# W1's half columns by token, with seven half products for eight, in a GLA and sliding-window decoder trunk on one core

## The chip, the core and the metric

The kernel runs on one core of a Trainium2 chip. The core has five engines with instruction queues of their own: TensorE (PE; its weight loads are shown apart as PEld), VectorE (DVE), ScalarE (ACT), GpSimd (POOL) and SyncE (SP). Weights come from DRAM through 16 DMA engines; transfers are issued from the queues of SP, ACT and POOL. The metric is the time of one execution on the device in microseconds (us).

## The reference

Two layers over 256 tokens of width 2048, fp32: a gated linear attention layer, then a sliding-window attention layer, each followed by an MLP of width 8192 with a squared relu. The change is in the MLPs:

```python
def sqrelu_mlp(h, w1, w2):
    u = jax.nn.relu(h @ w1)
    return (u * u) @ w2

def reference(x, norm_mix, norm_mlp, mlp_w1, mlp_w2, ...):
    h = x
    for layer in range(DEPTH):
        u = rmsnorm(h, norm_mix[layer])
        ...
        h = h + sqrelu_mlp(rmsnorm(h, norm_mlp[layer]), mlp_w1[layer], mlp_w2[layer])
    return h
```

## The kernel before

**Precision.** Every product of fp32 matrices is made of three matmuls in float32r: each operand is split into a rounded high part and the rest, and high x high, high x low and low x high are summed in PSUM. For weights `halve` (L105) does it: of a block of 512x512, held as [128, 4, 512] in `ws`, ACT casts two halves into `wh`, and DVE subtracts them into `wl`. This page calls such a pair of operations of one half "a cast". There are four `wh` halves and three `wl` and `ws` buffers, so the casts can be two blocks ahead of PE.

**The MLP.** `mlp` (L939) goes through the 8192 hidden columns in four groups of 2048 (`g`). In a group W1 comes first, in four pieces of 512 columns (`c`), by `gemm_wide` (L188): the weights are stationary, the 256 tokens move, with high and low part of the activations side by side, so that there are matmuls of 512 columns (high weights) and of 256 (low weights), 16 of each for a block of 512 rows of W1. The result has the hidden columns on the partitions. `evac_u` (L1136) sums, applies relu and the norm's scale `rb2`, and squares; for pieces 2 and 3 it splits the result into high and low part (`us`), for pieces 0 and 1 `combine` (L962) makes seven combinations of the token halves (`op`).

**Seven half products for eight.** W2 then comes in two `seven`s (L986), each for 1024 output columns. Of its rows, those of pieces 2 and 3 are multiplied plainly (`plain`: four blocks, 24 matmuls of 512 columns each). Those of pieces 0 and 1 form a 2x2 matrix of 512x512 blocks against a 2x2 matrix of token halves and row blocks, and are multiplied in seven half products (12 matmuls each) instead of eight, from sums of blocks and of activations. Sums of weight blocks are made in two ways: a DMA on POOL's queue that adds while it writes (`more`, L1002), or a sum on DVE. The same scheme stands in class `Seven` (L215) for the attention's V and R products and its output projection. There the steps run in an order given as a string: `1` to `7` are half products, `e` reads out two accumulators, and two digits such as `21` are a plain block (row block, column block). The seven products use the operands `es`, made from high and low parts by `combine_act` (L916) and `combinations` (L706).

In `Seven`, product 1 loads block (0,0) into `wx` (two halves of 512 KB), and `load_x` (L238) then adds block (0,1) onto it by two DMAs on POOL's queue, as soon as product 1's casts have read it. Product 5 uses that sum, and `load_x` adds block (1,1) for product 6. Product 3 loads (1,1) into `y`, product 7 sums it with (0,1) on DVE. Product 2 loads (1,0), which DVE adds to `wx` for product 4.

**Order.** The program is recorded step by step. `later(n, fn)` puts a function off until `n` calls of `tick` have passed (L70 to L78); blocks and products tick. Loads and casts are recorded with a priority that lets them move ahead of other work (`tc.high_priority`, L109); the framework's scheduler then fixes one order per engine. Each engine runs its instructions in that order and waits for semaphores of the others. PSUM has eight banks: four under the tag `acc`, two `tp`, two `ms`. The pool `actp` has eight buffers for activations; four hold the MLP's input (`act[0]` to `act[3]`, 512 model columns each) and four a group's `op` and `us`.

## Time and profile before

| what | us |
|---|---|
| median of three runs | 2032.58 |
| lowest and highest of them | 2032.13, 2032.89 |
| span of the profiled execution | 2031.4 |
| one group of an MLP (452.90 to 623.57) | 170.67 |
| of it: a wide piece of W1, four times | 22.19 |
| of it: a `seven` of W2, twice | 40.80 |

The profile is of one execution; its span runs from the first to the last instruction, and the medians of the runs are 1.2 us above it, which is what lies around a span. PE's granted clock is 1.00 throughout. In the profile's lists a row such as `L81 PE MATMUL acc<-wh,act` names the line, the engine, the operation, and the tiles written and read; in a chain or a timeline the first number is the start in the span and the second the length. A matmul's listed length is longer than its share of the pipeline, so the pace of matmuls is read from starts.

### The profile page before, as it was taken

What the parts mean: (1) busy time and instruction counts of PE and PEld (TensorE: products, weight loads), DVE (VectorE), ACT (ScalarE), POOL (GpSimd) and SP (SyncE); (2) the same over time, 40 slices, a digit from 0 to 9 for tenths busy, and PEclk for the clock granted to TensorE, in tenths of its full rate; (3) what the DMA queues carried; (4) which work ended last, traced back from release to release, by engine and by line L of the source; (5) the groups of instructions that cost most, each with busy time, mean ns of one, the idle gap of its engine ahead of it and who ended that gap; (6) DMA issues with size and microseconds to landing.
All of it is one profiled execution on the core that took longest, in us unless ns stands there. A gap on an engine that the chain in (4) does not pass through costs nothing.

```text
span 2031.4 us, 26969 instructions
## 1 busy us (share of the span) xinstructions
PE 2020.5 (99%) x10566; PEld 1715.5 (84%) x10566; DVE 1547.7 (76%) x1796; ACT 1203.8 (59%) x1638; POOL 162.4 (8%) x175
## 2 busy tenths in 40 slices
PE   9999999999999999999999999999999999999999
PEld 9988888888888888888888878788888888888887
DVE  6688787867876876786798676876876786787777
ACT  6746666656555655555567677655655555555555
POOL 2251110000000000000001121000000000000000
PEclk9999999999999999999999999999999999999999
DMA  8445876676875785786676543775785786687575
GB/s 286 146 156 177 227 208 200 194 251 184 261 236 187 228 267 189 203 253 219 187 220 186 165 146 126 198 257 188 227 268 188 203 253 221 186 256 231 187 223 148
DMA packets 219280, 423.15 MB, mean 208 GB/s; under 512 B 7328, under 2 KB 17840, under 8 KB 219152
## 3 DMA queue, kind: packets, MB, share of 16 engines
q1 hardware_dynamic: 194496, 376.73, 54.4%
q0 software_dynamic: 21568, 42.81, 12.3%
q10 hardware_dynamic: 3088, 1.88, 0.3%
q8 instruction: 83, 1.36, 0.3%
q14 instruction: 45, 0.37, 0.0%
HBM read 419.29 MB, written 2.10 MB: 207 GB/s over the span
## 4 chain that ended last, share of the span: by engine, by line
PE 91%; DVE 2%; issue 2%; DMA 2%; ACT 2%; SPq 0%; ACTq 0%; POOL 0%; POOLq 0%; DVEq 0%
PE acc L81 58%; PE ms L81 22%; PE tp L81 10%; DMA wx<-in_b_w_o_dram 1%; ACT sc L1283 1%; DVE wl L115 1%; PE tp L831 0%; DMA ws<-in_a_w_in_dram 0%; PE tp L1215 0%; DVE sc L1293 0%; DMA xt<-in_x_dram 0%; DVE st L1277 0%; PE tp L701 0%; ACT wh L114 0%; DVE qhl L1246 0%
## 5 line engine op out<-in xcount | busy, mean ns | idle before, releaser
L115 DVE TENSOR_TENSOR wl<-ws,wh 128x1024 fp32r<-128x1024 f32 x600 | 739.6, 1241 | 276.7 <-ACT wh L114 273.4
L114 ACT CAST wh<-ws 128x1024 fp32r<-128x1024 f32 x600 | 629.2, 1052 | 451.9 <-PE acc L81 286.6
L81 PE MATMUL acc<-wh,act 128*128 128x512 f32 x1696 | 543.9, 394 | 0.5 <-ACT act L339 0.5
L81 PE MATMUL acc<-act,wh 128*128 128x512 f32 (+1 forms) x1536 | 453.3, 358 | 0.7 <-ACT wh L401 0.7
L81 PEld LDWEIGHTS acc<-wh,act 128*128 128x128 f32 x1696 | 317.4, 188 | 68.6 <-issue 2.0
L81 PE MATMUL acc<-act,wl 128*128 128x256 f32 x1280 | 355.3, 279 | 0.4 <-DVE wl L402 0.2
L81 PE MATMUL acc<-wl,act 128*128 128x512 f32 x848 | 330.3, 390 | 0.0
L81 PEld LDWEIGHTS acc<-act,wh 128*128 128x128 f32 x1536 | 272.1, 189 | 44.0 <-ACT wh L401 0.9
L115 DVE TENSOR_TENSOR wl<-wx,wh 128x1024 fp32r<-128x1024 f32 x160 | 193.5, 1222 | 82.7 <-ACT wh L114 80.5
L114 ACT CAST wh<-wx 128x1024 fp32r<-128x1024 f32 x160 | 168.0, 1054 | 134.2 <-PE acc L81 76.7
L81 PEld LDWEIGHTS acc<-act,wl 128*128 128x128 f32 x1280 | 241.4, 189 | 2.4 <-DVE wl L402 1.0
L81 PE MATMUL tp<-act,wh 128*128 128x512 f32 x528 | 204.5, 392 | 0.9 <-DVE wh L518 0.9
L81 PE MATMUL ms<-act,wh 128*128 128x512 f32 x512 | 201.7, 394 | 0.0
L81 PEld LDWEIGHTS acc<-wl,act 128*128 128x128 f32 x848 | 159.4, 188 | 32.6 <-issue 1.4
L81 PE MATMUL ms<-wh,act 128*128 128x512 f32 x512 | 163.5, 390 | 0.0
L81 PE MATMUL ms<-act,wl 128*128 128x256 f32 x512 | 143.4, 280 | 0.0
L1004 POOL DMA_DIRECT2D wx<-in_mlp_w_dram x32 | 41.2, 1287 | 1265.5 <-DVE wl L115 1251.1
L81 PE MATMUL tp<-act,wl 128*128 128x256 f32 x512 | 141.1, 276 | 0.0
L81 PE MATMUL acc<-wh,op 128*128 128x512 f32 x384 | 123.4, 389 | 0.0
L81 PE MATMUL acc<-wh,ops 128*128 128x512 f32 (+1 forms) x392 | 123.2, 386 | 0.0
L81 PEld LDWEIGHTS tp<-act,wh 128*128 128x128 f32 x528 | 99.1, 188 | 24.2 <-DVE wh L518 1.2
L81 PEld LDWEIGHTS ms<-act,wh 128*128 128x128 f32 x512 | 95.7, 187 | 21.5
(278 smaller groups left out, 2551.6 us busy)
## 6 DMA issues: line engine op xcount, KB each, us to landing
ws<-in_mlp_w_dram SPq DMA_DIRECT2D x224, 1024.0 KB, 5.3
ws<-in_a_w_in_dram SPq DMA_DIRECT2D x42, 1024.0 KB, 5.1
wx<-in_mlp_w_dram POOLq DMA_DIRECT2D x32, 1024.0 KB, 9.0
wx<-in_mlp_w_dram SPq DMA_DIRECT2D x16, 1024.0 KB, 5.0
wy<-in_mlp_w_dram SPq DMA_DIRECT2D x16, 1024.0 KB, 7.5
ws<-in_b_w_q_dram SPq DMA_DIRECT2D x16, 1024.0 KB, 5.0
ws<-in_a_w_o_dram SPq DMA_DIRECT2D x15, 1024.0 KB, 5.1
ws<-in_b_w_o_dram SPq DMA_DIRECT2D x15, 1024.0 KB, 5.0
```

The costliest lines, as they stand in the source:

```text
L81: nc.tensor.matmul(o, lhsT=l, rhs=r, start=start, stop=stop, **kw)
L114: nc.scalar.copy(out=wh[:, js, :o], in_=w)
L115: nc.vector.tensor_sub(out=wl[:, ks, :o], in0=w, in1=wh.bitcast(F32)[:, js, :o])
L1004: nc.gpsimd.dma_start(out=ws, in_=block(i, j).rearrange("(k p) n -> p k n", p=P), accum_op=ALU.add)
L1283: nc.scalar.activation(out=sc[:, h], in_=sc[:, h], func=AF.Exp, bias=nmx[:, h:h + 1], scale=f[:, h:h + 1], accum_out=su[:, h:h + 1])
```

## The change

The first two pieces of W1 in each group are no longer made by `gemm_wide`. A new function `first_two` runs class `Seven` over them, with the tokens on the partitions: W1's rows of `act[0]` and `act[1]` go plainly, those of `act[2]` and `act[3]` in the seven half products (`skip=2` turns the row blocks by two). The four results (two token halves, two pieces) get relu and the norm's scale on ACT, are transposed by PE (`turn`: four 128x128 blocks each) and squared by ACT on the way back to `uf`.

The operands `es` from the activations are the same in all four groups. In the first group `combine_act` makes them at two ticks inside `first_two`, and SP writes them to two DRAM tiles (`kept`); in the other three groups two DMAs on POOL's queue read them back. `combine` for W2's operands is put off into piece 2. The first group has an order of its own, `FIRST`; the others use the second of `ORDERS`.

```diff
+FIRST = "21 31 1 20 30 3 7 e 5 6 2 4"
...
         def block(self, i, j):
-            return self.at(i, j).rearrange("(k p) n -> p k n", p=P)
+            return self.at((i + self.skip) % NC4, j).rearrange("(k p) n -> p k n", p=P)
...
         def p7(self, after):
             b12 = self.load(0, 1)
             with tc.high_priority(offset=WPRI):
                 nc.vector.tensor_add(out=b12, in0=b12, in1=self.y)
-            after["p7"](self.product("C", self.op(3), b12))
+            late = "C" in self.banks
+            after["p7"](self.product("D" if late else "C", self.op(3), b12))
+            if late:
+                self.banks.pop("D")
...
-    def combine_act(es, act, b, room):
+    def combine_act(es, act, b, room, cs=(0, 1)):
...
-        for c in range(2):
+        for c in cs:
...
+        dp = mx.enter_context(tc.tile_pool(name="dp", bufs=1, space=bass.MemoryType.DRAM))
+        kept = [dp.tile([P, 2, 2, 4, P], F32, name=f"kept{i}") for i in range(2)]
...
+        def first_two(g, uf):
+            pairs = [actp.tile([P, 2, 2, 4, P], F32R, name="cmb", tag="act") for _ in range(2)]
+            es = [a[:, i] for a in pairs for i in range(2)]
+            if g:
+                for a, o in zip(pairs, kept):
+                    with tc.high_priority(offset=WPRI):
+                        nc.gpsimd.dma_start(out=a.bitcast(F32), in_=o)
+            else:
+                for b in range(2):
+                    later(RS + 1 + 2 * b, lambda b=b: combine_act(es, act, b, room, (2, 3)))
+
+                def keep():
+                    for a, o in zip(pairs, kept):
+                        nc.sync.dma_start(out=o, in_=a.bitcast(F32))
+                later(RS + 4, keep)
...
+            def relu(o, i, t):
+                nc.scalar.activation(out=o, in_=i, func=AF.Relu, scale=r[:, t:t + 1])
+
+            def turn(c, t, h):
+                tp = bank([P, 4, P], "tp")
+                for k in range(4):
+                    nc.tensor.transpose(out=tp[:, k, :], in_=h[:, k * P:(k + 1) * P], identity=ident)
+                nc.scalar.activation(out=uf[c][:, :, t * P:(t + 1) * P], in_=tp, func=AF.Square)
+
+            def p56(p):
+                add(v, p, v)
+                add(x12, ef[0], v)
+                relu(x12, x12, 0)
+                later(1, lambda: turn(1, 0, x12))
+                if not g:
+                    add(x21, x21, x22)
+                sub(x22, v, x22)
+                add(x22, ef[1], x22)
+                relu(x22, x22, 1)
+                later(2, lambda: turn(1, 1, x22))
+                sub(x21, x21, v)
...
+            z = Seven(lambda i, j: w1[i * C:(i + 1) * C, g * D + j * C:g * D + (j + 1) * C], act, es,
+                      [x[:, 2 * i:2 * i + 2] for i in range(2)],
+                      lambda: mp.tile([P, 4, C], F32, name="wy", tag="wy", bufs=1), 2)
...
+                   "a": p2, "c": p4}, ORDERS[1] if g else FIRST)
...
         for g in range(4):
             w = w2[g * D:(g + 1) * D]
             us, op, uf = {}, None, {}
...
-            for c in range(NC4):
-                if c >= 2:
-                    us[c] = new_act()
-                elif c == 0:
-                    op = new_ops()
+            first_two(g, uf)
+            op = new_ops()
+            for odd in range(2):
+                later(3 + odd, lambda odd=odd, op=op, uf=dict(uf): combine(op, odd, uf))
+            later(1, lambda: pause(1))
+            for c in (2, 3):
+                us[c] = new_act()
```

What stands in the engines' rows now is seen at three places, all in the first group of the first layer's MLP. The first is PE. Before, a wide piece of W1 stood there (`acc` are its accumulators, `act` the activations, `wh` and `wl` the cast weights):

```order
L81 MATMUL acc_3728<-act_3396,wh_3797 128x512
L81 MATMUL acc_3728<-act_3396,wl_3798 128x256
L81 MATMUL acc_3729<-act_3396,wh_3797 128x512
L81 MATMUL acc_3729<-act_3396,wl_3798 128x256
L81 MATMUL acc_3726<-act_3760,wh_3837 128x512
```

Now, on PE, from the end of product 5 (`wh_4009`) through product 6 (`wh_4030`, `wh_4031`) into product 2 (`wh_4061`); `cmb_3725` holds the sums of activations, `tp_4007` is their accumulator:

```order
L82 MATMUL tp_4007<-wh_4009,cmb_3725 128x512
L82 MATMUL tp_4007<-wh_4030,cmb_3725 128x512
L82 MATMUL tp_4007<-wl_4032,cmb_3725 128x512
L82 MATMUL tp_4007<-wh_4030,cmb_3725 128x512 x2
L82 MATMUL tp_4007<-wl_4032,cmb_3725 128x512
L82 MATMUL tp_4007<-wh_4030,cmb_3725 128x512
L82 MATMUL tp_4007<-wh_4031,cmb_3725 128x512
L82 MATMUL acc_3826<-wh_4061,act_3672 128x512
L82 MATMUL tp_4007<-wl_4032,cmb_3725 128x512
```

All are matmuls of 512 columns with the weights moving, and product 6 follows product 5 directly, with one matmul of product 2 ahead of its last third. The second place is DVE. Before, in the middle of the second wide piece, it had casts alone:

```order
L115 TENSOR_TENSOR wl_4039<-ws_4035,wh_4038 128x1024
L115 TENSOR_TENSOR wl_4080<-ws_4076,wh_4078 128x1024
L115 TENSOR_TENSOR wl_4080<-ws_4076,wh_4079 128x1024
L115 TENSOR_TENSOR wl_4157<-ws_4153,wh_4155 128x1024
L115 TENSOR_TENSOR wl_4157<-ws_4153,wh_4156 128x1024
```

Now, on DVE, from just before product 5's cast (`wl_4010`) to product 2's (`wl_4063`); `e`, `m` and `cmb` are `combine_act`'s sums, `wx_3727` the block that the DMAs add to:

```order
L714 TENSOR_TENSOR e_3914<-m_3911,e_3913 128x256
L116 TENSOR_TENSOR wl_4010<-wx_3727,wh_4008 128x1024
L714 TENSOR_TENSOR cmb_3725<-e_3913,cmb_3725 128x256
L116 TENSOR_TENSOR wl_4010<-wx_3727,wh_4009 128x1024
L714 TENSOR_TENSOR cmb_3725<-e_3913,cmb_3725 128x256
L714 TENSOR_TENSOR cmb_3726<-e_3914,cmb_3726 128x256 x2
L116 TENSOR_TENSOR wl_4032<-wx_3727,wh_4030 128x1024
L981 TENSOR_TENSOR h_3729<-h_3729,h_3728 128x512
L324 TENSOR_TENSOR wx_3727<-wx_3727,ws_4057 128x1024
L116 TENSOR_TENSOR wl_4032<-wx_3727,wh_4031 128x1024
L116 TENSOR_TENSOR wl_4063<-ws_4057,wh_4061 128x1024
```

The sums of activations stand between the casts, and the cast of product 6 (`wl_4032`), which needs the block that was added to, stands ahead of those of products 2 and 4. The third place is POOL's queue. Before, behind the norm's power came W2's accumulates alone:

```order
L347 TENSOR_TENSOR rstd_2917<-rv_3765,mhalf_103 128x2
L1004 DMA wx_4524<-in_mlp_w2_dram 128x4x512 x2
L1004 DMA wx_4814<-in_mlp_w2_dram 128x4x512 x2
L1004 DMA wx_5875<-in_mlp_w2_dram 128x4x512 x2
L1004 DMA wx_6165<-in_mlp_w2_dram 128x4x512 x2
```

Now, on POOL, through the first group and into the second:

```order
L352 TENSOR_TENSOR rstd_2917<-rv_3766,mhalf_103 128x2
L245 DMA wx_3727<-in_mlp_w1_dram 128x2x512 x3
L1078 DMA wx_4531<-in_mlp_w2_dram 128x4x512 x2
L1078 DMA wx_4821<-in_mlp_w2_dram 128x4x512 x2
L967 DMA cmb_5111<-kept0_3723 128x2048
L967 DMA cmb_5112<-kept1_3724 128x2048
L245 DMA wx_5115<-in_mlp_w1_dram 128x2x512 x4
```

Each group has four accumulating DMAs of W1 more (one of the first group's stands ahead of the power), and from the second group on two reads of `kept` stand behind the last accumulates of the group before.

## The prediction

> **What bounds the kernel now.** First the page's head, with the busy shares by engine, and its fourth part, the chain of work that ended last, by engine.

> ```profile
> span 2031.4 us, 26969 instructions
> PE 2020.5 (99%) x10566; PEld 1715.5 (84%) x10566; DVE 1547.7 (76%) x1796; ACT 1203.8 (59%) x1638; POOL 162.4 (8%) x175
> ...
> PE 91%; DVE 2%; issue 2%; DMA 2%; ACT 2%; SPq 0%; ACTq 0%; POOL 0%; POOLq 0%; DVEq 0%
> ```

> TensorE (PE) is busy for 99% of the span and is 91% of that chain. So time goes only where PE gets less to do, and comes only where PE is made to wait. Next the chain in order of time over one group of 2048 MLP columns (start, length, what), and the same stretch as windows (span; then busy time of PE, weight loads, DVE, ACT, POOL; granted clock, DMA share, GB/s).

> ```profile
> 452.90 22.19 PE acc L81 x128
> ...
> 500.03 13.60 PE ms L81 x60
> ...
> 452.90:475.09 22.19, 22.19 (x129) 19.57 (x129) 17.02 (x23) 13.32 (x21) 0.00 (x0) 1.00 0.58 190
> ...
> 500.03:540.83 40.80, 40.80 (x182) 33.78 (x181) 35.74 (x34) 25.03 (x26) 2.58 (x2) 1.00 0.77 243
> ```

> A wide piece, 512 columns of W1, is 128 matmuls in 22.19 us, without a gap. Sixty matmuls of 512 columns take 13.60 us: 0.2267 us each. The last row is one `seven` of W2: four plain blocks of 24 matmuls and seven half products of 12, together 180, and 180 x 0.2267 = 40.8. It too has no gap, though DVE is busy for 35.74 us of it. `first_two` has the same 180 matmuls and nearly the same casts and sums.

> **What goes.** Two wide pieces per group, 2 x 22.19 = 44.38 us of PE, become 40.80: 3.58 us less, in eight groups (four per layer) 28.6 us. The two pieces' evacuation on ACT and DVE goes too, off the path.

> **What comes on PE.** Four `turn`s of four fp32 transposes per group. The nearest rows are the residual's transposes between full matmuls (start, length, what).

> ```profile
> 1055.37 0.60 PE L831 MATMUL tp<-ident,xs 128*128 128x128 f32 x4
> 1055.73 0.48 PE L81 MATMUL ms<-wh,act 128*128 128x512 f32 x1
> ...
> 1058.59 0.60 PE L831 MATMUL tp<-ident,xs 128*128 128x128 f32 x4
> ```

> From one four to the next are 3.22 us, and twelve matmuls between them are worth 2.72: 0.5 us for four. At least it is the 0.36 us to the next start, at most four times the 0.27 us of a single one, 1.1. I take 0.5, the steady figure: 2.0 us per group, 16.0 in all (bounds 11.5 and 35). PE alone thus gives 28.6 - 16.0 = 12.6 us, 0.62%, if nothing waits.

> **What comes in an MLP's first group.** Here the order is `FIRST`: ... 3 7 e 5 6 2 4. Product 5 casts `wx`, then `load_x` adds block (1,1) onto it with two DMAs on POOL's queue, and product 6 casts the sum. `FIRST` puts 5 and 6 side by side, where the residual keeps two plain blocks (20 and 30) between them. What that interval is worth is seen in the second residual: the POOL issue, ACT's cast of product 6, DVE's work behind it, and the view of L243 with its landings.

> ```profile
> 1314.31 2.44 POOL L243 DMA_DIRECT2D wx<-in_b_w_o_dram  x2 [21.07 <-DVE wl L115]
> ...
> 1326.17 1.05 ACT L114 CAST wh<-wx 128x1024 fp32r<-128x1024 f32 x1 [4.08 <-DMA wx<-in_b_w_o_dram]
> ...
> 1315.43 10.64 DMA wx<-in_b_w_o_dram
> ...
> DMA to landing us min/median/max: 5.8/6.3/10.6
> ...
> wx<-in_b_w_o_dram POOLq DMA_DIRECT2D x2, 512.0 KB, 8.4
> ```

> ACT waited 4.08 us for the second half's landing, 10.6 us after its issue, although two blocks (10.9 us of PE) stood between; two megabytes of weights were on their way beside it. In the new order nothing stands between, and 2 MB of sums on their way to `kept` are beside it: the situation of these rows, so I take their median, 8.4 us, with 5.8 and 10.6 as ends.

> When does the accumulate start? DVE carries more in this group, since `combine_act` of chunks 2 and 3 stands between product 1 and product 5. Its operations by their rows (line, shapes, count; busy, mean ns):

> ```profile
> L115 DVE TENSOR_TENSOR wl<-wx,wh 128x1024 fp32r<-128x1024 f32 x160 | 193.5, 1222 | 82.7 <-ACT wh L114 80.5
> L114 ACT CAST wh<-wx 128x1024 fp32r<-128x1024 f32 x160 | 168.0, 1054 | 134.2 <-PE acc L81 76.7 <-PE ms L81 34.9 <-DMA wx<-in_mlp_w_dram 8.2
> L925 DVE TENSOR_TENSOR xu<-act 128x512 f32<-128x512 f32 x8 | 5.5, 686 | 3.2 <-PE ms L81 2.1 <-PE tp L701 1.0
> L709 DVE TENSOR_TENSOR xe<-xu,xe 128x256 f32<-128x256 f32 x12 | 5.0, 419 | 0.0
> L319 DVE TENSOR_TENSOR wx<-wx,ws 128x1024 f32<-128x1024 f32 x8 | 9.8, 1226 | 0.3
> L1085 DVE TENSOR_TENSOR wy<-wy,ws 128x2048 f32<-128x2048 f32 x16 | 36.6, 2286 | 0.1
> ...
> 1320.79 0.68 DVE L896 TENSOR_TENSOR xs<-acc,xs 128x512 f32<-128x512 f32 x1
> 1321.39 0.68 DVE L896 TENSOR_TENSOR xs<-tp,xs 128x512 f32<-128x512 f32 x1
> ```

> Operations in a row start 0.08 us sooner than their lengths add up (1320.79 to 1321.39 is 0.60, not 0.68), so a cast counts 1.14, a 512-wide sum 0.60, a 256-wide one 0.34, the sum of two whole blocks 2.2. From the start of product 1 up to the first half of product 5's cast DVE has eight casts (9.1), four sums of 512 (2.4), twelve of 256 (4.1), two rows of `along` (0.4) and one whole-block sum (2.2): 18.2 us. PE has product 1 and two plain blocks in that time, 2.72 + 10.88 = 13.6. So the cast ends 4.6 us after PE starts product 3. Without backlog it would wait only for a `wh` buffer: half a product (1.36), ACT's cast (1.05), its own (1.14), 3.6 us.

> From there: landing 4.6 + 8.4 = 13.0; ACT casts till 14.05; then DVE has, in its order, six casts, two `wx` sums and one sum of 512 up to the last cast of product 4 (8 x 1.14 + 0.60 = 9.7, till 23.8), and PE the five matmuls behind that (1.1): 24.9. Six products in a row would be 16.3. **PE loses 8.6 us**, 4.9 with the early cast and the shortest landing (3.6 + 5.8 + 1.05 + 9.7 + 1.1 - 16.3), 10.8 with the longest. Wide piece 2 then finds its buffers empty: DVE owes its first two casts, a sum and one cast of the next block (3 x 1.14 + 0.60 = 4.0 us), PE has 2.5 us (the five matmuls and eight of the wide piece): 1.5 us more, bounds 0 and 3. Together 10.1 per first group, **20.2 us** in both layers.

> **What comes in the other groups.** There 20 and 30 stand between 5 and 6 and the path stays PE's. In 6 2 4 DVE has six sums of 512 (3.6 us) beside its casts and `wx` sums; counted in the same way, the sum of `x21`, which frees the fourth accumulator bank, ends some 0.5 us after PE wants it behind product 4. With the transposes' relu on ACT I take 0.6 (0 to 2): 3.6 us in six groups. `combine` now stands wholly in piece 2 (eleven operations of 0.60 = 6.6 us). With 8 casts (9.1) and six late sums (3.6) DVE has 19.3 us there beside 24 of PE: hidden; without that cover it would cost up to 6.6 per group. The reloads of `kept` on POOL's queue wait for PE's last use of `us`, at the latest the end of the last plain block of the group before; three products, two plain blocks and product 1 (8.2 + 13.6 = 21.8 us) run before product 3 reads them.

> ```profile
> ws<-in_mlp_w_dram SPq DMA_DIRECT2D x224, 1024.0 KB, 5.3
> wx<-in_mlp_w_dram POOLq DMA_DIRECT2D x32, 1024.0 KB, 9.0
> ...
> 408.50:430.70 22.20, 22.20 (x135) 19.62 (x134) 14.83 (x23) 12.39 (x22) 0.72 (x1) 1.00 0.98 343
> ```

> A megabyte on that queue took 9.0 us (on SP's 5.3), so they cost nothing. The further 2 MB of weights per group also hide: 12 MB in 42.8 us are 280 GB/s, and the last row shows 343 with PE full. Writing `kept` stands on SP's queue between two weight loads and is ready for both soon after product 5's cast; nothing on PE waits for the write alone.

> **The sum.** -28.6 + 16.0 + 20.2 + 3.6 = +11.2 us on the profiled 2031.4. The median of the runs, 2032.58, is 1.2 us above that span, which is taken along: 2043.8, say **2044 us**, +0.6%. It is slower by two waits that the first groups buy with a gain meant for all eight.

> **Rivals.** (1) *The accumulate lands early.* With the early cast, a landing of 5.8 and no backlog behind it, a first group waits 4.9: 9.8 + 16.0 - 28.6 + 0 = -2.8, 2030 us; with 3.6 for the later groups 2033. For it: half of the L243 landings are under 6.3. Against: twelve small sums stand ahead of the cast in DVE's order. [...]

> (2) *Product 6 is covered, and the change is faster.* One mechanism, at the step from 5 to 6: if cast plus landing fit under the products still queued, the sum is -12.6 + 0 to 4, 2020 to 2024 us. It decides at 4.2 us per first group: more, and what is left of 12.6 is within 0.2% (4.1 us, about what a measurement of this kernel tells from no change). Cast plus landing would have to be 7.2 us (7.2 + 1.05 + 9.7 + 1.1 - 16.3 = 2.7, and 1.5 behind it); the shortest by the rows is 9.4.

> (3) *The wait grows.* If weights land late in the six other groups as well (their two reloads beside 10 MB of blocks), say two loads by 1.2 us, it is 14 us more: 2058. It begins where a block takes longer than the three products that it is asked for ahead, 8.2 us; the median is 5.3. Or PE's clock falls: every row above has it at 1.00, and PE nowhere stands still for long. With half the clock over products 6, 2 and 4 (5.44 us each for the 3.3 at which DVE feeds them) the two first groups would lose some 4.3 each: 2052. [...] No row here can show it.

> **Chances.** My sum 0.58, with a range of its own from 2037 to 2052; (1) 0.17; (2) 0.08; (3) 0.17. So faster by over 0.2% 0.08, within it 0.17, slower 0.75. For 8 in 10 the range leaves (2) out and the end of (3): 2030 to 2060, which also holds the first groups' waits from 4.9 to 10.8 + 3.

> **What would show it.** In the profile after: a group but the first takes some 169.7 us instead of 170.7 (3.58 less, 2.0 for transposes, 0.6 of waiting); in each first group the chain leaves PE between products 5 and 4, with the DMA to `wx` and then a row of DVE casts, some 10 us together; the POOL landing there is near 8 us; the four transposes stay near 0.5 us. It is wrong if PE goes through 5 6 2 4 without a gap, if the groups' period falls by far less than 1 us, or if waits on `cmb` show at product 3 of later groups.

## The result, and the profile after

The changed kernel takes 2051.26 us (median of four runs, 2050.33 to 2054.12) where the kernel before takes 2032.74: a ratio of 1.0093, with a 95% interval from 1.0078 to 1.0107. It is slower, as forecast, by 18.5 us instead of 11.2. Its profiled execution took 2050.72, with a span of 2049.0, which is 17.6 above the span before. The head of the page and its fourth part, the chain by engine:

```profile
span 2049.0 us, 26361 instructions
PE 2020.6 (99%) x10082; PEld 1694.0 (83%) x10082; DVE 1641.3 (80%) x1862; ACT 1267.2 (62%) x1694; POOL 208.9 (10%) x219
...
PE 89%; DMA 3%; DVE 3%; ACT 2%; issue 2%; SPq 0%; POOL 0%; ACTq 0%; POOLq 0%; DVEq 0%
```

PE's busy time has not moved (2020.6 for 2020.5), although it has 484 matmuls fewer: a half clock and slower wide pieces, both shown below, fill most of what they left. In the chain PE has lost two per cent, and DMA and DVE have gained one each. Where the time went is seen from the starts of one landmark, the sixty `ms` matmuls in the first `seven` of each group (chain of work, after):

```profile
513.01 13.60 PE ms L82 x60
...
682.15 13.60 PE ms L82 x60
...
852.02 13.60 PE ms L82 x60
...
1021.17 13.60 PE ms L82 x60
...
1454.17 13.60 PE ms L82 x60
...
1623.32 13.60 PE ms L82 x60
```

| landmark of group | before | after | later by | this group's share |
|---|---|---|---|---|
| layer 1, first | 500.03 | 513.01 | 12.98 | +12.45 (0.53 was there ahead of the MLP) |
| second | 670.69 | 682.15 | 11.46 | -1.52 |
| third | 841.35 | 852.02 | 10.67 | -0.79 |
| fourth | 1012.01 | 1021.17 | 9.16 | -1.51 |
| layer 2, first | 1432.21 | 1454.17 | 21.96 | +12.80 |
| second to fourth | 1944.19 (fourth) | 1961.60 | 17.41 | -1.52 each |
| end | 2031.4 | 2049.0 | 17.6 | |

The two first groups cost 25.3 us, and the six others bring back 8.4. In the first group of layer 1 PE's timeline shows the waits, in brackets with who ended them; the first row is the start of product 3, the last that of wide piece 2:

```profile
433.63 0.39 PE L82 MATMUL acc<-wh,cmb 128*128 128x512 f32 x1
...
438.30 0.50 PE L82 MATMUL acc<-wh,cmb 128*128 128x512 f32 x1 [1.35 <-ACT cmb L720]
...
446.92 0.50 PE L82 MATMUL tp<-wh,cmb 128*128 128x512 f32 x1 [3.10 <-ACT h L1021]
...
453.36 0.79 PE L82 MATMUL tp<-wh,cmb 128*128 128x512 f32 x1 [3.82 <-ACT wh L115]
...
462.58 0.39 PE L82 MATMUL acc<-act,wh 128*128 128x512 f32 x1
```

Products 3, 7, 5, 6, 2 and 4 take 28.95 us where their matmuls are worth 16.3: 12.65 lost. The two long waits are at the two halves of product 6, and behind both stands the accumulating DMA: first the rows of POOL and SP, then ACT's, then DVE's.

```profile
438.64 1.21 POOL L245 DMA_DIRECT2D wx<-in_mlp_w_dram  x1 [19.19 <-DVE wl L116]
440.10 1.20 POOL L245 DMA_DIRECT2D wx<-in_mlp_w_dram  x1 [0.26 <-DVE wl L116]
...
440.17 1.01 SPq L974 DMA_DIRECT2D kept<-cmb  x2
...
444.85 1.04 ACT L115 CAST wh<-wx 128x1024 fp32r<-128x1024 f32 x1 [6.29 <-DMA wx<-in_mlp_w_dram]
...
446.27 0.59 ACT L1021 COPY h<-tp 128x512 f32<-128x512 f32 x1
452.26 1.04 ACT L115 CAST wh<-wx 128x1024 fp32r<-128x1024 f32 x1 [5.40 <-DMA wx<-in_mlp_w_dram]
...
453.33 1.23 DVE L116 TENSOR_TENSOR wl<-wx,wh 128x1024 fp32r<-128x1024 f32 x1 [4.45 <-ACT wh L115]
454.48 1.22 DVE L116 TENSOR_TENSOR wl<-ws,wh 128x1024 fp32r<-128x1024 f32 x1
...
460.15 2.45 DVE L116 TENSOR_TENSOR wl<-ws,wh 128x1024 fp32r<-128x1024 f32 x2
```

The first half was issued at 438.64 and could be cast at 444.85, 6.2 us later; the second, issued at 440.10, at 452.26, 12.2 us later. The write of the sums to `kept` (L974), 2 MB, was issued right behind the second, at 440.17. PE's start at 446.92 hung on one thing more: product 6 sums into the bank of product 5, ACT copies product 5's sum out of it (L1021), and that copy stands in ACT's order behind the cast that waits for the first landing. From 453.33 DVE works through its casts without a gap, and PE follows with no wait over 0.15 us, until 457.7 at half its clock. The windows (span; busy PE, weight loads, DVE, ACT, POOL; granted clock, DMA share, GB/s) show the transfers and the clock:

```profile
406.00:421.00 15.00, 14.96 (x75) 12.33 (x74) 12.90 (x22) 11.12 (x22) 3.38 (x3) 1.00 0.94 329
421.00:436.00 15.00, 14.73 (x67) 11.69 (x66) 14.97 (x22) 8.61 (x13) 0.00 (x0) 1.00 0.98 285
...
442.00:448.00 6.00, 2.90 (x11) 1.99 (x11) 2.08 (x3) 2.02 (x3) 0.00 (x0) 0.95 1.05 327
448.00:453.00 5.00, 1.53 (x4) 0.66 (x2) 0.88 (x1) 0.74 (x1) 0.00 (x0) 0.50 0.75 206
```

The DMA engines are nearly full from the MLP's start to the wait (0.78 from 436 to 439), and DVE is full from 421 to 436. The clock goes to 0.50 behind the first wait; its records have that state from 447.4 for 10.24 us, in layer 2 from 1392.9 for 6.83.

### The profile page after: what moved, and what is told of

Same layout as the page of the kernel before. It is cut to its first block, busy times and chain, and to the rows that moved or that the text cites. A ratio compares the mean times of both kernels' runs of the same rounds, so it can differ in the third digit from the quotient of the medians.

```text
span 2049.0 us, 26361 instructions
## 1 busy us (share of the span) xinstructions
PE 2020.6 (99%) x10082; PEld 1694.0 (83%) x10082; DVE 1641.3 (80%) x1862; ACT 1267.2 (62%) x1694; POOL 208.9 (10%) x219
## 3 DMA queue, kind: packets, MB, share of 16 engines
q0 software_dynamic: 32000, 72.18, 18.6%
## 4 chain that ended last, share of the span: by engine, by line
PE 89%; DMA 3%; DVE 3%; ACT 2%; issue 2%; SPq 0%; POOL 0%; ACTq 0%; POOLq 0%; DVEq 0%
PE acc L82 62%; PE ms L82 18%; PE tp L82 7%; DMA wx<-in_mlp_w_dram 3%; ACT sc L1355 1%; PE tp L990 1%; DVE wl L116 1%; DMA ws<-in_a_w_in_dram 1%; ACT wh L115 0%; PE tp L836 0%; DVE sc L1365 0%; PE tp L1287 0%; DVE st L1349 0%; PE tp L706 0%; DVE po L1382 0%
## 5 line engine op out<-in xcount | busy, mean ns | idle before, releaser
L115 ACT CAST wh<-ws 128x1024 fp32r<-128x1024 f32 x568 | 595.0, 1051 | 361.6 <-PE acc L82 248.8
L82 PE MATMUL acc<-wh,act 128*128 128x512 f32 x2400 | 767.8, 394 | 0.8 <-ACT act L344 0.5
L82 PEld LDWEIGHTS acc<-wh,act 128*128 128x128 f32 x2400 | 450.6, 188 | 98.2 <-ACT wh L115 2.0
L82 PE MATMUL acc<-wl,act 128*128 128x512 f32 x1200 | 468.1, 390 | 0.0
L116 DVE TENSOR_TENSOR wl<-wx,wh 128x1024 fp32r<-128x1024 f32 x224 | 270.8, 1222 | 126.0 <-ACT wh L115 122.1
L115 ACT CAST wh<-wx 128x1024 fp32r<-128x1024 f32 x224 | 235.0, 1054 | 197.8 <-PE acc L82 88.6
L82 PE MATMUL acc<-act,wh 128*128 128x256 f32 (+1 forms) x1024 | 277.6, 342 | 1.0 <-ACT wh L406 1.0
L82 PE MATMUL acc<-act,wl 128*128 128x256 f32 x768 | 214.9, 283 | 0.0
L82 PEld LDWEIGHTS acc<-act,wh 128*128 128x128 f32 x1024 | 177.1, 191 | 21.8 <-ACT wh L406 1.3
L115 ACT CAST wh<-wy 128x1024 fp32r<-128x1024 f32 x80 | 84.3, 1054 | 60.2 <-PE ms L82 50.4
L82 PEld LDWEIGHTS ms<-wh,act 128*128 128x128 f32 x512 | 96.1, 188 | 19.9
L116 DVE TENSOR_TENSOR wl<-wy,wh 128x1024 fp32r<-128x1024 f32 x80 | 96.4, 1221 | 18.9 <-ACT wh L115 16.9
L82 PE MATMUL tp<-act,wh 128*128 128x512 f32 x272 | 104.7, 394 | 0.2 <-DVE wh L523 0.2
L82 PE MATMUL ms<-act,wh 128*128 128x512 f32 x256 | 100.8, 394 | 0.0
L82 PE MATMUL ms<-wl,act 128*128 128x512 f32 x256 | 99.6, 389 | 0.0
## 6 DMA issues: line engine op xcount, KB each, us to landing
ws<-in_mlp_w_dram SPq DMA_DIRECT2D x208, 1024.0 KB, 6.1
ws<-in_a_w_in_dram SPq DMA_DIRECT2D x42, 1024.0 KB, 5.1
wx<-in_mlp_w_dram POOLq DMA_DIRECT2D x32, 1024.0 KB, 9.4
wy<-in_mlp_w_dram SPq DMA_DIRECT2D x24, 1024.0 KB, 7.5
wx<-in_mlp_w_dram SPq DMA_DIRECT2D x16, 1024.0 KB, 6.4
wx<-in_mlp_w_dram POOLq DMA_DIRECT2D x32, 512.0 KB, 9.1
ws<-in_b_w_q_dram SPq DMA_DIRECT2D x16, 1024.0 KB, 5.0
ws<-in_a_w_o_dram SPq DMA_DIRECT2D x15, 1024.0 KB, 5.1
```

What stands on the lines that cost most here:

```text
L82: nc.tensor.matmul(o, lhsT=l, rhs=r, start=start, stop=stop, **kw)
L115: nc.scalar.copy(out=wh[:, js, :o], in_=w)
L116: nc.vector.tensor_sub(out=wl[:, ks, :o], in0=w, in1=wh.bitcast(F32)[:, js, :o])
```

## The experiments

Each ratio is against the kernel before on the same chip, with its 95% interval.

**keep_after6**: the write of the sums moved behind product 6, held there by two one-column operations that need its result.

```diff
-                later(RS + 4, keep)
...
                 add(x22, ef[1], x22)
+                if not g:
+                    for a in pairs:
+                        a1 = a[:, 0, 0, 0, 0:1]
+                        nc.vector.scalar_tensor_tensor(out=a1, in0=v[:, 0:1], scalar=0.0, in1=a1.bitcast(F32),
+                                                       op0=ALU.mult, op1=ALU.add)
+                    keep()
```

> Only the write of the activation sums to DRAM is moved, from beside the accumulate of block (1,1) to behind product 6. Theory A, the 2 MB write stretches that accumulate: its second half lands 6 to 9 us after its issue instead of 12.1, PE's wait before the second half of product 6 falls from 3.8 and 4.7 us to under 1, its clock stays at 1.00, and each first group is 3.5 to 6.5 us shorter: 2038 to 2044 us. Rival B, the accumulate is slow by itself or by the weight loads beside it: the second half still lands after 11 to 12 us and the time is 2049 to 2052.

It took 2044.87 us, 1.0056 (1.0041 to 1.0071). Its timeline, POOL, then ACT, then PE:

```profile
437.12 1.21 POOL L245 DMA_DIRECT2D wx<-in_mlp_w_dram  x1 [18.53 <-DVE wl L116]
438.93 1.20 POOL L245 DMA_DIRECT2D wx<-in_mlp_w_dram  x1 [0.60 <-DVE wl L116]
...
445.99 1.04 ACT L115 CAST wh<-wx 128x1024 fp32r<-128x1024 f32 x1 [1.00 <-DMA wx<-in_mlp_w_dram]
...
448.83 0.57 ACT L1026 COPY h<-tp 128x512 f32<-128x512 f32 x1
...
448.03 0.80 PE L82 MATMUL acc<-wh,act 128*128 128x512 f32 x1 [5.65 <-ACT wh L115]
449.46 0.80 PE L82 MATMUL tp<-wh,cmb 128*128 128x512 f32 x1 [0.63 <-ACT h L1026]
```

The second half now lands 7.1 us after its issue instead of 12.2, as theory A said, and the time is just outside its range: 3.2 us per first group came back. The rest was kept by a new order. The scheduler put a matmul of product 2 ahead of product 6, and the copy of product 5's sum behind the casts of product 2's block, so PE waits 5.65 us in one piece; and the clock still falls (half for 6.83 and 10.24 us). So the write makes the landing late; the order on ACT can keep PE waiting without that.

**no_acc**: the first group does without the sum with block (1,1).

```diff
...
             p = self.product("D", self.op(0), self.wx)
-            self.load_x(1, 1)
+            if not self.bare:
+                self.load_x(1, 1)
...
+            z.bare = not g
```

> Left out: in the first group of each MLP block (1,1) is not added to the buffer, so product 6 uses what product 5 used (and product 4's sum lacks that block). Theory A, the landing is what PE waits for in the first groups: the waits of 3.0 and about 4.3 us and the half clock behind them go, 9 to 11 us per first group, 2029 to 2033 us. Rival B, DVE's backlog of casts would hold PE in any case: less than 4 us per first group come back, over 2043.

It took 2032.10, 0.9994 (0.9985 to 1.0004): 19.2 us less, 9.6 per first group. PE's waits in the first group of layer 1 (PE tile and line, who ended it, total, times, longest):

```profile
PE tp L82 <- ACT h L1023: 1.4, 1, 1.4
PE acc L82 <- ACT cmb L721: 1.3, 1, 1.3
```

The accumulate is what a first group waits for, and without it the loss against the kernel before is gone. DVE's backlog alone doesn't hold PE so long. Not all that a first group loses is gone: the span is 2030.9, and without any wait it would be 2031.4 - 12.6 = 2018.8, so some 5 us per first group remain (an estimate; 1.7 us are taken off for what lies elsewhere, as in the changed kernel).

**plain_between** and **k6_between**: a plain block moved between products 5 and 6; and that together with the later write.

```diff
-FIRST = "21 31 1 20 30 3 7 e 5 6 2 4"
+FIRST = "21 31 1 20 3 7 e 5 30 6 2 4"
```

> FIRST is "21 31 1 20 3 7 e 5 30 6 2 4": a plain block (5.44 us) moves from ahead of product 3 to between products 5 and 6. Theory A, product 6 then waits less by 5.4 us, but products 3 and 7 come 5.4 us earlier to activation sums that DVE does not have earlier, and wait for them some 3 to 5 us: 1 to 4 us per first group come back, 2043 to 2049 us, with waits on cmb. Rival B, the sums are there in time: 5.4 us and the half clock come back in each first group, 2035 to 2041 us.

> Both moves together: the write of the sums stands behind product 6, and plain block 30 between products 5 and 6. Theory A, the two waits for the second half of the accumulate (11.2 us to its landing and 3.0 and 4.3 us of PE's waiting in plain_between) are the write's doing: the second half lands 6 to 9 us after its issue, under block 30, no wait over 1.5 us is left at product 6, the granted clock stays at 1.00 in the first groups, and 3 to 5 us per first group come back on 2045.5: 2035 to 2040 us. Rival B, DVE's casts would hold PE there anyway: under 1.5 us per first group, 2042 to 2046 us.

plain_between took 2045.48, 1.0062 (1.0047 to 1.0077), k6_between 2035.46, 1.0012 (1.0003 to 1.0022). In plain_between the accumulate is issued earlier (436.00), but still lands 11.2 us later:

```profile
447.34 1.04 ACT L115 CAST wh<-wx 128x1024 fp32r<-128x1024 f32 x1 [4.89 <-DMA wx<-in_mlp_w_dram]
...
449.40 0.50 PE L82 MATMUL tp<-wh,cmb 128*128 128x512 f32 x1 [2.98 <-ACT h L1021]
```

The wait for the sums of activations was 1.43 us, less than theory A's 3 to 5; the landing took up what the block between gave (PE still waits 2.98 us, in the second layer 4.32). In k6_between the view of L245 for the same stretch, and ACT's cast of the second half:

```profile
DMA to landing us min/median/max: 7.6/8.0/8.4
...
445.28 1.05 ACT L115 CAST wh<-wx 128x1024 fp32r<-128x1024 f32 x1 [0.85 <-DMA wx<-in_mlp_w_dram]
```

The landing is all but hidden (in the second layer it is 8.3 and 9.1 us, and PE waits 0.82 us), and 5.0 us more per first group came back. Together the two moves take back 15.8 of the 18.5 us. One part of theory A failed: the clock fell once more, for 3.41 us.

**no_sums**: DVE's sums for the first groups left out, ACT casts activations in their place.

```diff
...
-                    later(RS + 1 + 2 * b, lambda b=b: combine_act(es, act, b, room, (2, 3)))
+                    later(RS + 1 + 2 * b, lambda b=b: cast_only(b))
```

> Left out: DVE's 32 sums for the seven products' activations in the first groups; ACT casts parts of the activations in their place (16 casts of 256 columns). Theory A, that work on DVE delays product 5's casts and so the accumulate's issue, by about 1 to 2 us, and product 7 by 1.35 us: 2 to 4 us per first group come back, 2043 to 2047 us. Rival B, only the landing and what ACT has queued behind it count: less than 1 us per first group, 2049 to 2052 us.

It took 2047.85, 1.0077 (1.0062 to 1.0092), between the two theories. Why so little comes back is the useful part. Without the sums the write is ready early: it was issued at 425.49, 12 us ahead of the accumulate (437.41, 1.2 us earlier than in the changed kernel). The window in which it ran, the landings of the accumulate, and those of the two weight loads to `ws` that were issued behind the write (428.2 and 435.8):

```profile
421.00:436.00 15.00, 14.45 (x66) 11.69 (x66) 10.11 (x9) 10.92 (x19) 0.00 (x0) 1.00 1.06 341
...
DMA to landing us min/median/max: 9.0/10.3/11.7
...
DMA to landing us min/median/max: 12.2/13.7/15.2
```

The landing stays at 9.0 and 11.7 us, although the write had landed by 436.8 (9.1 us after its second issue at 427.7). So it isn't that the write is issued beside the accumulate: the loads behind it took 12.2 and 15.2 us (9.4 and 5.1 for the nearest two in the changed kernel), and the accumulate lands among them. In this stretch, whose DMA engines are full (1.06), 2 MB more make late what stands behind them, the accumulate too. In keep_after6 it was issued behind product 6, at 460.53 (in the changed kernel the DMA share was 0.37 from 453.36 to 462.60), and no cost of it was seen there.

**warm** and **warm_gap**, for the clock: matmuls of no use in PE's idle time. In warm 31 stand ahead of the halves of product 6; in warm_gap three between them, and they read product 5's copied sum (the diff is warm_gap's).

```diff
...
+                if k == 2 and fill is not None:
+                    pt = small()
+                    for _ in range(3):
+                        mm(pt, ident, fill)
...
+            z.fill = None if g else x21
```

> In each first group 31 matmuls of no use (7.0 us, 512 columns each) stand ahead of the two halves of product 6, where PE idled 8.3 us, so that it is never idle for 3 us. Theory A, the half clock behind the idle time costs time of its own: the granted clock is 1.00 throughout, and the time falls by 2 to 3 us per first group less up to 0.5 us that the added matmuls hold product 6 back, 2045 to 2048 us. Rival B, DVE's casts set PE's pace there at either clock: 2050 to 2053.

> Three fp32 matmuls of no use stand in the first groups between the two halves of product 6; they read product 5's copied sum, so the order on every engine is that of the changed kernel otherwise. Theory A, the idle time there halves the clock behind it, and that costs 1.5 to 3 us: in the second layer (idle 2.95, then 4.74 us) the clock stays at 1.00 and the first group is 1.5 to 3 us shorter; in the first layer, where the clock falls before the added matmuls, it changes by less than 2 us; 2047 to 2050 us. Rival B, DVE's casts set the pace behind the gap at either clock: the second layer's first group changes by less than 0.7 us.

warm took 2059.69, 1.0133 (1.0116 to 1.0150), slower by 8.4 for another reason than either theory's: product 5's copy slid behind the cast of the second half on ACT, and PE waited 8.1 and 8.9 us in one piece. It shows the price of that order, not of the clock. warm_gap took 2047.29, 1.0075 (1.0059 to 1.0090); its profiled execution was the longest of its four, 2050.36, hardly less than the changed kernel's 2050.72. Both were run again, side by side:

> The changed kernel once more, beside warm_gap_2 on one chip: 2049 to 2053 us.

> The kernel of warm_gap once more, to separate what its profile and its median left apart (0.35 us less in the profile, 4.0 us less in the median). Theory A, the half clock behind product 6's idle time costs 1.5 to 3 us per first group: 3 us or more under after_2 in the median. Rival B, DVE's casts set the pace there: within 1.5 us of after_2.

They took 2049.49, 1.0081 (1.0067 to 1.0094), and 2050.28, 1.0085 (1.0072 to 1.0099). So the changed kernel took 2051.26 and then 2049.49, and what an experiment takes back, counted here from 2051.26, is uncertain by about 0.9 us per first group. In the windows of warm_gap PE has its full clock where the changed kernel had 0.77 (453.36 to 462.60) and 0.50 (1395 to 1399), and DVE is full all the same. Behind them stand two rows of PE in the second layer, a wait for DVE in product 6 and the start of wide piece 2:

```profile
453.40:462.60 9.20, 8.05 (x34) 6.12 (x35) 9.20 (x9) 7.72 (x9) 0.00 (x0) 1.00 0.39 123
...
1394.00:1403.00 9.00, 7.62 (x31) 5.76 (x32) 8.77 (x8) 7.63 (x9) 0.00 (x0) 1.00 0.33 101
...
1395.51 0.50 PE L82 MATMUL tp<-wl,cmb 128*128 128x512 f32 x1 [0.76 <-DVE wl L116]
...
1402.90 0.39 PE L82 MATMUL acc<-act,wh 128*128 128x512 f32 x1
```

Rival B stands for the time: at its full clock PE waits for DVE instead (0.76 us here, and 0.37 later), and in the medians the two kernels are 4.0 us apart one way and 0.8 the other. The traces do show a smaller price. From ACT's cast of the second half to wide piece 2 it is 9.75 to 9.77 us in the three first groups with a full clock in that stretch (both of warm_gap, one of its repeat), and 9.97 to 11.47 in the five others (both of the changed kernel, twice, and one of the repeat). Up to the landmark it is 60.7 against 59.9 to 61.9. On average that is 1.0 us per first group at wide piece 2 and 0.3 at the landmark, less than theory A's 1.5 to 3. The order was not quite the same: in warm_gap one of DVE's sums stands behind the casts and holds wide piece 2 by 0.3 us.

**no_turn**: the transposes left out.

```diff
-                tp = bank([P, 4, P], "tp")
-                for k in range(4):
-                    nc.tensor.transpose(out=tp[:, k, :], in_=h[:, k * P:(k + 1) * P], identity=ident)
-                nc.scalar.activation(out=uf[c][:, :, t * P:(t + 1) * P], in_=tp, func=AF.Square)
+                nc.scalar.activation(out=uf[c][:, :, t * P:(t + 1) * P], in_=h.rearrange("p (k n) -> p k n", k=4),
+                                     func=AF.Square)
```

> Left out: the sixteen transposes of each group; ACT squares the untransposed sums into the same places. Theory A, the transposes are plain time of PE at 0.5 us for four: a later group's period falls from 169.15 to 167.1 us (3.58 less than before the change), and the whole by 16 to 16.5 us, to 2034 to 2036 us. Rival B, part of them lies in time in which PE would wait anyway for DVE's sums: the period falls by less than 1.2 us and the time stays over 2041.

It took 2037.21, 1.0021 (1.0011 to 1.0031): 14.1 us less, for 16 expected. A later group's period (chain, the 120 matmuls that follow the landmark) is 167.86, not 167.1:

```profile
523.57 27.20 PE acc L82 x120
...
691.43 27.20 PE acc L82 x120
```

What is missing has a place. The matmuls of a wide piece run at one of two paces; 30 us of them in the second and in the third group of the changed kernel:

```profile
643.00:673.00 30.00, 30.00 (x175) 26.43 (x175) 21.48 (x27) 16.48 (x22) 0.00 (x0) 1.00 0.58 184
813.00:843.00 30.00, 30.00 (x172) 26.00 (x171) 20.93 (x26) 15.92 (x22) 0.00 (x0) 1.00 0.59 188
```

175 against 172 matmuls, the clock at 1.00 and PE never idle in both; the third group's period is 169.87, the second's 169.14, so the slow pace costs 0.73 us per group. In no_turn the three later groups of either layer have the slow one. With 0.73 taken off, the period is 167.13, and the transposes cost 2.01 per group, 0.50 us for four. That correction is worked out, not run by itself.

**wide_first**, from what the others showed: the first group of each MLP keeps its four wide pieces, and makes and writes the sums under its second one.

```diff
             else:
                 for b in range(2):
-                    later(RS + 1 + 2 * b, lambda b=b: combine_act(es, act, b, room, (2, 3)))
+                    later(RS + 5 + 2 * b, lambda b=b: combine_act(es, act, b, room, (2, 3)))
...
-                later(RS + 4, keep)
+                later(RS + 8, keep)
+                return
...
-            for c in (2, 3):
+            for c in (2, 3) if g else range(NC4):
...
```

> The first group of each MLP has four wide pieces again, the sums of the activations are made and written to DRAM in its second wide piece, and only the other three groups use the seven half products for W1. Theory A, the later groups keep 1.52 us each and the first groups cost nothing: 2032.6 - 6 x 1.52 + 0.7 (one slower group) = 2024 us, range 2022 to 2026. Rival B, the sums on DVE and the write beside full wide pieces cost PE up to 6.6 us per first group: 2028 to 2037.

> The kernel of wide_first once more, in five rounds: 2024 to 2027 us, 0.3 to 0.4% below the kernel before.

It took 2025.95, 0.9967 (0.9955 to 0.9978), and in the second set 2024.89, 0.9959 (0.9946 to 0.9973): faster than both kernels. By the spans it is 7.6 us, about six times 1.52 less 1.4, since two of the six later groups took 0.7 us longer. The windows of its second and third wide piece:

```profile
427.50:450.00 22.50, 22.50 (x132) 19.67 (x132) 20.74 (x37) 14.01 (x25) 0.00 (x0) 1.00 0.54 164
450.00:472.00 22.00, 22.00 (x129) 19.26 (x128) 17.81 (x23) 13.22 (x20) 0.00 (x0) 1.00 0.87 317
```

DVE has room for the sums there (20.74 of 22.5 us), the DMA engines have room for the write (0.54, then 0.87), and PE doesn't wait.

## Why the prediction was right in direction and 7 us short

- **The gain, -3.58 per group: right.** A later group is 1.52 us shorter, which is 3.58 less the transposes' 2.01, and 0.05 that is left over.
- **The transposes, 0.5 us for four: right**, with the correction above 0.50; without it 0.32, which is below the bound of 0.36.
- **The first groups' wait, 10.1 each: right in place and kind, too small.** The first half's cast ended 4.7 us after product 3's start (predicted 4.6). The term that was too small is the landing. I took both halves as one transfer at their median, 8.4 us, with 10.6 as the longest, and counted it from the first cast: 13.0 us after product 3's start. The second half counts; it was issued 6.5 us after product 3's start and took 12.2, so its data were there at 18.6. Of these 5.6 us, 1.9 are the later issue and 3.8 the longer landing. From there to the end of product 4 it was 10.3 us instead of 11.9, since the first half's casts were done by then: 12.65 lost instead of 8.6. Wide piece 2 found its buffers full, so the 1.5 behind didn't come; 0.7 us of slow pace did. In either first group 0.3 to 0.6 us are assigned to nothing.
- **"The situation of these rows"** held in kind, and was misread. The 8.4 is the middle of two landings, 6.2 us for the residual's first half and 10.6 for its second; here, to the landing itself, they are 6.1 and 12.1. With the longest the prediction has 10.8, and 13.8 with its bound for the piece behind, close to the 14.2 measured, but by other terms. keep_after6 (7.1 us) shows that the write is what makes the second half late; why 12.1 and not 10.6 was not separated. That nothing on PE waits for the write alone held.
- **The later groups' 0.6 each: mostly not there.** PE has no wait in them that the timeline shows; one of the six has the slow pace (0.73).
- **Hidden work: right.** No wait on `cmb` at product 3 of later groups; wide_first's sums and write hide as well.

By these terms the span is -28.6 + 16.1 + 2 x 14.2 (12.45 and 12.80, each 1.6 more without the gain), + 0.3 + 0.7 for the later groups and + 0.7 outside the MLPs' groups: +17.6, as measured. Of the rivals, the early landing and the covered product 6 were wrong for this order. The third was right that the clock falls: no row of before shows the half that its sum uses (1.00 throughout), and the changed kernel then had 0.50 at product 6, from 447.4 and from 1392.9. But it hit the time (2052) by luck: its 4.3 us per first group are the 2.1 us of two products, where it names three (6.4), and warm_gap and its repeat leave about 1. The price of the half clock was that small because DVE for the most part set the pace behind the gap: it was busy for all of the 9.20 us from 453.40 in warm_gap, at the full clock.

In k6_between a first group still takes some 6 us more than before (landmarks at 507.51, of which 1.72 were there ahead of the MLP, and 1441.28, with 3.07 there at the landmark of the group before). DVE's sums, the short waits at products 3, 7 and 2 and the slow pace are all there; they weren't separated.

## What to carry to other kernels

A step that needs its set-up once (here the sums, their write and the tight order) is best given its first use where the set-up has cover; it may be cheaper to leave the first of several passes in the old form (2025.95 us in wide_first, for 2051.26). The landing time of a transfer is read from a stretch with the same load on the DMA engines, and of a transfer in halves the last half counts (12.2 us here, where the residual's median was 8.4). Where an engine runs in order, look at what stands behind an instruction that waits for a DMA: the copy that freed a PSUM bank stood there (PE waited for it 3.10 us in the changed kernel, 8.1 and 8.9 in warm), and one of the experiments (warm) got slower and one (keep_after6) gained less by it.

## What had not been expected of the hardware

```profile
442.91:446.32 3.41, 1.72 (x7) 0.89 (x6) 3.41 (x4) 2.65 (x4) 0.00 (x0) 1.00 0.75 315
446.32:449.74 3.42, 3.42 (x10) 2.67 (x9) 2.82 (x3) 1.04 (x1) 0.00 (x0) 0.50 0.04 9
```

In k6_between it was 1.67 of 3.42 us. So these half clocks came without waits as long as the changed kernel's (3.10 and 3.82 us). The recorded half clocks last 3.41, 6.83 or 10.24 us, and the two of the changed kernel start 945.49 us apart, 277 times a third of 10.24. How busy PE was ahead of them is read from the eleven traces whose first groups have the seven half products (all but wide_first and its repeat). Their first groups, cut into windows of 3.41 us that start where the recorded half clocks start, give this: of the windows at full clock each of the twenty with at most 1.17 us busy was followed by a half clock, and none with 1.82 or more was; from 1.60 to 1.76 both occurred, three times each. In the changed kernel the windows from 444.02 (0.52 us busy) and 1389.51 (0.00) were followed by one, those from 1382.68 (1.67) and 1386.10 (1.73) were not.

The two paces of the wide pieces (one pair of matmuls in 0.347 or 0.353 us by their starts, held through both pieces of a group) have no cause that these runs show.
